# Stacking both directions of a gated linear attention state into one product, and reordering the decays, loads and norms around it

## The chip, the cores and the metric

The kernel runs on one core of a Trainium2 chip. The metric is the device time of one execution in microseconds (us), lower is better. PE is the matrix engine, PEld its weight loads, DVE, ACT and POOL the vector, scalar and general engines, SP the engine whose queue issues most DMAs.

## What is computed

The reference is one step of a two-layer backbone over 2048 latent tokens and 128 context tokens. The part that the change touches is the bidirectional gated linear attention (GLA) of the first layer: four heads, keys of 64, values of 128, a decay per token and key, a state S (64x128) per head and direction. Cut to that part:

```python
def gla_chunked(q, k, v, g, s0):              # one direction
    def step(S, inp):
        qc, kc, vc, gc = inp
        b = jnp.cumsum(gc, axis=2)
        o_inter = jnp.einsum('bhcd,bhde->bhce', qc * jnp.exp(b), S)
        diff = b[:, :, :, None, :] - b[:, :, None, :, :]
        decay = jnp.where(causal, jnp.exp(jnp.where(causal, diff, 0.0)), 0.0)
        att = jnp.einsum('bhid,bhjd,bhijd->bhij', qc, kc, decay)
        o = o_inter + jnp.einsum('bhij,bhje->bhie', att, vc)
        b_last = b[:, :, -1:, :]
        S_new = jnp.exp(b_last)[:, :, 0, :, None] * S + jnp.einsum('bhcd,bhce->bhde', kc * jnp.exp(b_last - b), vc)
        return S_new, o
    ...

o_f, s_f = gla_chunked(q, k, v, gf, s0f)
o_b, s_b = gla_chunked(flip(q), flip(k), flip(v), flip(gb), s0b)
o = rmsnorm(o_f + flip(o_b), gla_onorm)       # per head
y_gla = o * silu(z_gla)
out = concat([y_gla, y_s5]) @ w_out           # then x = x + gate * out, and the next layer's norm
```

## The kernel before

Tokens are cut into 17 tiles of 128: tiles 0 to 15 are latent, tile 16 is the context, which reads no state. The GLA works on tiles as chunks. `run` first does the S5 branch and the input products, then `gla_back` (L913), then `phase4` (L1155), then the second layer.

`gla_back` walks from tile 16 and then from 15 to 1 and computes the backward states. Each step loads keys, decays and values, forms decayed keys (POOL, ACT, DVE), calls `kv_update` (L944) for the key-value product, and adds it to the decayed state (L939, two DVE operations). All 16 backward states stay in SBUF in `self.sb`, 16 KB a partition, in the pool `glac` on the left side, with the first forward state `sf0` (1 KB). A step of `gla_back` is woven with dense products (`zg_pass`, and `glu_pass` with its stores `zg_d` and `ys_d` on POOL's queue).

`kv_update` transposes the decayed keys (L949, two transposes), copies them (L951) and makes four products, one a head, of 64 output columns each (L955). Heads alternate between output partitions 0 to 63 and 64 to 127 by `tile_position=(0, o)`, and two pairs of heads lie one behind the other.

`phase4` runs a loop over the tiles, written by `weave` (L1577): in round i, `gla_chunk(i)` is the main generator, and at each of its nine steps one step is taken of `turn(i-1)` (norm output transposed, L1179, gated, split for the product), `gla_pre(i+1)` (preparation of the next chunk) and `after(i-2)` (output projection by `out_proj`, residual, row norm, `make_h` with eight transposes, L243, and stores). A planner orders the instructions of every engine from this program by a model of their times, so the order on an engine is not the program's; data and buffers are kept consistent by semaphores.

`gla_pre` loads `qk`, `B` (the summed log decays) and `v`, makes the decayed keys `kh`, and with L1035 to L1038 the decayed queries `qh` of both directions, laid out as 64 rows a head and direction. It calls `gla_arg` for levels 0 to 2 and updates the forward state (L1054). `gla_arg` (L987) makes the decay arguments of one level: four POOL operations (L1003 to L1006), an exponential on ACT (L1007) and a DVE product (L1008). The last level is only a product of queries and keys on POOL (L995).

`gla_chunk` (L1057) has eight levels. In a level, four products of 64 rows (L1081) give scores for that distance of tokens, and a copy by mask (L1088) puts them into `att`. The arguments of the level two ahead are issued at each level. Then, per head, come the product with the forward state (L1096), with the backward state (L1097), and with the values (L1098), all into one accumulator; a copy to `gy` (L1100), four squares (L1105), the inverse root on DVE (`rsqrt`, L83: eleven small operations) and the scaling on POOL (L1107). The row norm of `after` has an inverse root of its own (L1195) and scales the row tile on DVE (L1196).

## Time and profile before

| | before |
|---|---|
| median of 3 runs | 2409.3 us (2407.95 to 2409.64) |
| profiled execution, time | 2415.59 us |
| profiled execution, span | 2413.7 us |
| mean granted clock of PE, as a share of full speed | 0.966 |
| PE busy | 2268.3 us, 94% |
| DVE busy | 1659.3 us, 69% |
| ACT busy | 1042.7 us, 43% |
| POOL busy | 867.6 us, 36% |
| DMA | 332.90 MB, mean 138 GB/s |

The span runs from the first to the last instruction. Matmuls are pipelined and their recorded durations overlap, so the cost of a product is read from the start of one instruction to the start of the next. A product of 32-bit floats outside the split form of `mm3` has two records, a transpose has one.

### The profile page before, as it was taken

The numbers are of one execution on the slowest core, as the hardware profiler recorded it, in microseconds if no ns is written. First come the engines' busy times: TensorE is split into PE (matmuls) and PEld (weight loads), VectorE is DVE, ScalarE is ACT, GpSimd is POOL, SyncE is SP. The second block draws the span as 40 slices with busy tenths as digits, with TensorE's granted clock in tenths as the row PEclk, the third lists the DMA queues.
The fourth block names the chain that finished last, engine by engine and source line by source line (L and its number), as shares of the span: only waits on it lengthen the run. The fifth ranks groups of instructions, "written<-read, shape, count | busy, mean of one in ns | idle before, by whom it ended". The sixth has DMA issues, their size and how long they took to land.

```text
span 2413.7 us, 47276 instructions
## 1 busy us (share of the span) xinstructions
PE 2268.3 (94%) x17473; PEld 2108.3 (87%) x17473; DVE 1659.3 (69%) x3916; ACT 1042.7 (43%) x2533; POOL 867.6 (36%) x1348
## 2 busy tenths in 40 slices
PE   7999887888899987999999999999999997999998
PEld 4988787887897876888888999999999997999998
DVE  4997688888866776888887665565344336676765
ACT  3554644343544453455454432233122115565653
POOL 4127165566522227767674021111101102222221
PEclk9999988999999995999999999999999998999999
DMA  9765853343469873333333642245133223222221
GB/s 322 236 210 181 252 162 99 102 132 110 131 212 310 291 232 100 123 119 123 116 115 102 210 120 80 80 138 147 50 93 102 68 69 100 88 89 88 90 69 58
DMA packets 328040, 332.90 MB, mean 138 GB/s; under 512 B 43969, under 2 KB 274977, under 8 KB 327809
## 3 DMA queue, kind: packets, MB, share of 16 engines
q1 hardware_dynamic: 265312, 238.84, 33.1%
q0 software_dynamic: 14384, 48.65, 5.9%
q10 hardware_dynamic: 48112, 42.38, 5.4%
q8 instruction: 138, 2.26, 0.4%
q14 instruction: 94, 0.76, 0.1%
HBM read 223.57 MB, written 106.22 MB: 137 GB/s over the span
## 4 chain that ended last, share of the span: by engine, by line
PE 57%; DVE 8%; issue 4%; DMA 4%; ACT 2%; POOL 2%; SPq 0%; ACTq 0%; POOLq 0%; DVEq 0%
PE psD L100 7%; PE psW L100 7%; PE psW L101 7%; PE psW L102 7%; PE psD L102 7%; PE psD L101 7%; PE psP L1081 3%; PE psW L1510 2%; PE psW L1463 2%; DVE tabs L641 2%; PE psT L1498 2%; PE psP L1098 1%; PE psP L1096 1%; DMA wst<-in_w_in_o_dram 1%; DMA wst<-h_d 1%
## 5 line engine op out<-in xcount | busy, mean ns | idle before, releaser
L100 PE MATMUL psD<-slot,yT 128*128 128x256 f32 x1088 | 318.2, 293 | 1.9 <-ACT yT L1125 1.9
L102 PE MATMUL psD<-slot,yT 128*128 128x256 f32 x1088 | 314.1, 292 | 0.0
L101 PE MATMUL psD<-slot,yT 128*128 128x256 f32 x1088 | 310.7, 286 | 0.0
L101 PE MATMUL psW<-hq,slot 128*128 128x272 f32 x1024 | 293.0, 287 | 0.0
L102 PE MATMUL psW<-hq,slot 128*128 128x272 f32 x1024 | 292.9, 287 | 0.0
L100 PE MATMUL psW<-hq,slot 128*128 128x272 f32 x1024 | 289.1, 287 | 0.0
L100 PE MATMUL psD<-hq,slot 128*128 128x272 f32 x768 | 235.1, 308 | 46.8 <-ACT fo L814 45.8
L101 PE MATMUL psD<-hq,slot 128*128 128x272 f32 x768 | 230.0, 300 | 0.0
L102 PE MATMUL psD<-hq,slot 128*128 128x272 f32 x768 | 229.5, 300 | 0.0
L100 PEld LDWEIGHTS psD<-slot,yT 128*128 128x128 f32 x1088 | 208.1, 191 | 10.0 <-ACT yT L1125 2.0
L102 PEld LDWEIGHTS psD<-slot,yT 128*128 128x128 f32 x1088 | 205.8, 191 | 4.5 <-issue 2.2
L101 PEld LDWEIGHTS psD<-slot,yT 128*128 128x128 f32 x1088 | 208.1, 191 | 1.8
L100 PEld LDWEIGHTS psD<-hq,slot 128*128 128x128 f32 x768 | 151.8, 199 | 55.2 <-ACT fo L814 48.8
L102 PEld LDWEIGHTS psW<-hq,slot 128*128 128x128 f32 x1024 | 193.1, 189 | 0.0
L101 PEld LDWEIGHTS psW<-hq,slot 128*128 128x128 f32 x1024 | 192.5, 188 | 0.0
L100 PEld LDWEIGHTS psW<-hq,slot 128*128 128x128 f32 x1024 | 190.6, 188 | 0.0
L641 DVE SCALAR_TENSOR_TENSOR tabs<-tabs,s5A,tabw 128x16 f32<-128x16 f32 (+2 forms) x384 | 146.8, 447 | 24.9 <-ACT tabw L637 23.5
L101 PEld LDWEIGHTS psD<-hq,slot 128*128 128x128 f32 x768 | 152.1, 198 | 6.4 <-issue 4.7
L102 PEld LDWEIGHTS psD<-hq,slot 128*128 128x128 f32 x768 | 152.1, 198 | 1.0 <-issue 1.0
L1472 DVE CUSTOM_DVE_ANT_0 sc<-psW,amask,sink 128x512 f32<-128x512 f32 (+1 forms) x128 | 93.6, 732 | 84.7 <-PE psT L1498 76.2
L1007 ACT ACTIVATE arg<-arg 128x512 f32<-128x512 f32 x119 | 75.0, 631 | 143.6 <-POOL arg L1006 140.3
L1475 ACT ACTIVATE sc<-sc,nm 128x512 f32<-128x512 f32 (+1 forms) x128 | 90.9, 710 | 87.9 <-DVE nm L1474 74.8
(376 smaller groups left out, 6543.2 us busy)
## 6 DMA issues: line engine op xcount, KB each, us to landing
wst<-h_d SPq DMA_DIRECT2D x96, 272.0 KB
hq<-hl_d SPq DMA_DIRECT2D x40, 544.0 KB
hl_d<-ht POOLq DMA_DIRECT2D x17, 1024.0 KB, 6.7
wada<-in_w_ada_dram SPq DMA_DIRECT2D x32, 512.0 KB
h_d<-hf SPq DMA_DIRECT2D x17, 512.0 KB
x_d<-x ACTq DMA_DIRECT2D x17, 512.0 KB
h_d<-hf ACTq DMA_DIRECT2D x17, 512.0 KB
wst<-h_d SPq DMA_DIRECT2D x34, 256.0 KB
```

Of the source, the lines that this page charges most:

```text
L100: mm(out, lh, rh, start=start, stop=False)
L101: mm(out, lh, rl, start=False, stop=False)
L102: mm(out, ll, rh, start=False, stop=stop)
L641: V.scalar_tensor_tensor(x[:, at(d, m)], x[:, at(d, 0)], turn(0, d, gg), w[:, 1 - j], op0=OP.mult, op1=op)
L1007: nc.scalar.activation(arg, arg, AF.Exp, scale=0.0625)
L1081: nc.tensor.matmul(pv[:, hh, pr, :], ak[o : o + 64, pr, :], aq[o : o + 64, pr, :], start=True, stop=True)
L1096: nc.tensor.matmul(ot, qh[o : o + 64, 0, pr, :], sf[o : o + 64, pr], start=True, stop=False)
L1463: nc.tensor.matmul(out, r32(qs[:, j, h]), kk, start=j == 0, stop=j == 1)
L1472: V.tensor_tensor_reduce(sv, ps, mask, 1.0, sk[:, h : h + 1], op0=OP.add, op1=OP.max, accum_out=m)
L1475: nc.scalar.activation(sv, src, AF.Exp, bias=nm[:, h : h + 1], accum_out=sm[:, h : h + 1])
L1498: nc.tensor.transpose(pt[:, c, :], t[:, 128 * c : 128 * c + 128], self.ident)
L1510: nc.tensor.matmul(po[kv][:, j % 2], r32(VV[:, b, kv]), r32(t[:, x, :, c, :]), start=c + x == 0, stop=c + x == nb)
```

## The change

- The states of both directions lie in one tile: forward at partitions 0 to 63, backward at 64 to 127, four heads side by side. The decayed queries are stacked in the same way, so that a head's product with both states is one product of 128 rows.
- For this `kv_update` puts all four heads at one output position, 0 in `gla_pre` and 64 in `gla_back`. `next_state` multiplies the old state by its decay on POOL and adds the product on DVE.
- `gla_back` keeps two states and stores each to DRAM (`sb_d`) by a DMA on POOL's queue; `state` loads the backward half for the chunk. The pool `glac` is gone.
- `gla_queries` loads queries and decays in the stacked layout with six DMAs a chunk, two chunks ahead.
- `gla_pre` calls `gla_arg` for levels 0 to 3, and `gla_chunk` for the level three ahead; the buffers of levels above 1 are five.
- The head norm (`gla_norm`) is issued in `turn`, in the round after its chunk, and its inverse root has a fifth column for a row tile of `after`, whose scaling (now on ACT), transposes and store are issued there (`rows`). `x1` has three buffers. The sum of squares of a row tile is scaled by 1/8 to share the divisor 128.

```diff
@@ -926,22 +927,32 @@
             nc.gpsimd.tensor_tensor(E, B[:, :, 0:1].to_broadcast([128, 2, 128]), B, op=OP.subtract)
             nc.scalar.activation(E, E, AF.Exp, scale=0.0625)
             nc.vector.tensor_tensor(E, E, k, op=OP.mult)
-            kv = self.kv_update(p, E, v)
+            kv = self.kv_update(p, E, v, 64)
             if i == 16:
...
+                st = p.tile([128, 4, 128], F32, name="bs", tag="bs", bufs=2)
+                nc.sync.dma_start(st[64:128], a["s0"][1])
                 yield
                 continue
-            eb = p.tile([128, 2], F32, name="beb", tag="beb")
-            nc.scalar.activation(eb, B[:, :, 0], AF.Exp, scale=0.0625)
-            for pr in range(2):
-                nc.vector.scalar_tensor_tensor(
-                    self.sb[:, i - 1, pr], self.sb[:, i, pr], eb[:, pr : pr + 1], kv[:, pr], op0=OP.mult, op1=OP.add
-                )
+            eb = p.tile([128, 2, 2], F32, name="beb", tag="beb")
+            for hh in range(2):
+                nc.scalar.activation(eb[64:128, :, hh], B[64 * hh : 64 * hh + 64, :, 0], AF.Exp, scale=0.0625)
+            nst = p.tile([128, 4, 128], F32, name="bs", tag="bs", bufs=2)
+            self.next_state(p, slice(64, 128), nst, st, eb, kv)
+            st = nst
+            nc.gpsimd.dma_start(self.sb_d[i - 1], st[64:128])
             yield
 
-    def kv_update(self, p, kd, v):
+    def next_state(self, p, o, dst, src, eb, kv):
+
+        t = p.tile([128, 4, 128], F32, name="dst", tag="dst", bufs=1)
+        e = eb.rearrange("p a b -> p (a b)")[o].unsqueeze(2).to_broadcast([64, 4, 128])
+        self.nc.gpsimd.tensor_tensor(t[o], src[o], e, op=OP.mult)
+        self.nc.vector.tensor_tensor(dst[o], t[o], kv, op=OP.add)
+
+    def kv_update(self, p, kd, v, o):
 
         nc = self.nc
         pt = self.bank("T", (128, 2, 128))
...
@@ -949,16 +960,11 @@
             nc.tensor.transpose(pt[:, pr, :], kd[:, pr, :], self.ident)
         kt = p.tile([128, 2, 128], F32, name="kt", tag="kt", bufs=2)
         nc.scalar.copy(kt, pt)
-        kv = self.bank("T", (128, 2, 128))
+        kv = self.bank("T", (128, 4, 128))[o : o + 64]
         for h in range(4):
-            pr, o = h // 2, 64 * (h % 2)
+            pr, c = h // 2, 64 * (h % 2)
             nc.tensor.matmul(
-                kv[o : o + 64, pr, :],
-                kt[:, pr, o : o + 64],
-                v[:, h * 128 : h * 128 + 128],
-                start=True,
-                stop=True,
-                tile_position=(0, o),
+                kv[:, h], kt[:, pr, c : c + 64], v[:, h * 128 : h * 128 + 128], start=True, stop=True, tile_position=(0, o)
             )
         return kv
 
...
@@ -980,7 +986,8 @@
         self.ga = {t: Ring(ga, gc) for t in ("qk", "B", "v")}
         self.ga["arg"] = [ga, gb]
         self.gp = self.pool(es, "glap", 2, side="right")
-        self.gs = {}
+        self.ss, self.xrow = self.gp.tile([128, 5], F32, name="oss", tag="oss", bufs=3), None
+        self.gs, self.gq, self.gn = {}, {}, {}
 
     STEPS = (64, 32, 16, 8, 4, 2, 1, 0)
 
...
@@ -995,7 +1002,7 @@
             G.tensor_tensor(st[li], qk[:, 0], qk[:, 1], op=OP.mult)
             return
         nb = 256 // (2 * s)
-        arg = self.ga["arg"][li > 1].tile([128, 2, 256], F32, name="arg", tag="arg", bufs=4 if li > 1 else 2)
+        arg = self.ga["arg"][li > 1].tile([128, 2, 256], F32, name="arg", tag="arg", bufs=5 if li > 1 else 2)
         av = arg.rearrange("p j (b e s) -> p j b e s", e=2, s=s)
         bv = [B[:, d].rearrange("p r (b e s) -> p (r b) e s", e=2, s=s) for d in range(2)]
         rf = bv[0][:, :, 0, s - 1 : s].to_broadcast([128, nb, s])
...
@@ -1019,8 +1026,17 @@
         for j in range(2):
             nc.sync.dma_start(qk[:, j], self.qk_d[256 * j : 256 * j + 256, ts].rearrange("(r p) t -> p r t", p=128))
             nc.sync.dma_start(B[:, j], self.b_d[:, j, :, ts].rearrange("r p t -> p r t"))
+        if i < 16:
+            if i == 0:
+                self.state(0)
+                nc.sync.dma_start(self.sf[0:64], a["s0"][0])
+            st["sf"] = self.sf
         v = st["v"] = self.ga["v"].tile([128, 512], F32, name="v", tag="v", bufs=1)
         nc.sync.dma_start(v, self.v_d[ts, :])
+        if i == 0:
+            self.gla_queries(0)
+        if i < 15:
+            self.gla_queries(i + 1)
         yield
         self.gla_arg(i, 0)
         yield
...
@@ -1030,42 +1046,59 @@
         V.tensor_tensor(kh, kh, qk[:, 1], op=OP.mult)
         yield
         qa = self.ha.tile([128, 2, 2, 272], F32, name="hq", tag="hq").rearrange("p a b c -> p (a b c)")
-        qh, st["att"] = (qa[:, 512 * j : 512 * j + 512].rearrange("p (a b c) -> p a b c", a=2, b=2) for j in range(2))
-        st["qh"] = qh
-        nc.scalar.activation(qh, B, AF.Exp, scale=0.0625)
-        eb = p.tile([128, 2], F32, name="eb", tag="eb")
-        V.tensor_copy(eb, qh[:, 0, :, 127])
-        V.tensor_tensor(qh, qh, qk[:, 0:1].to_broadcast([128, 2, 2, 128]), op=OP.mult)
+        st["att"] = qa[:, 0:512].rearrange("p (a b c) -> p a b c", a=2, b=2)
+        if i < 16:
+
+            qh, qq = self.gq.pop(i)
+            st["qh"] = qh
+            eb = p.tile([128, 2, 2], F32, name="eb", tag="eb")
+            nc.scalar.activation(eb[0:64].rearrange("p a b -> p (a b)"), qh[0:64, :, 127], AF.Exp, scale=0.0625)
+            nc.scalar.activation(qh, qh, AF.Exp, scale=0.0625)
+            V.tensor_tensor(qh, qh, qq, op=OP.mult)
         yield
         self.gla_arg(i, 1)
         yield
         self.gla_arg(i, 2)
         yield
-        sf = st["sf"] = self.sf
+        self.gla_arg(i, 3)
         if i != 15:
-            kv = self.kv_update(p, kh, v)
+            kv = self.kv_update(p, kh, v, 0)
             if i == 16:
...
             else:
-                self.sf = p.tile([128, 2, 128], F32, name="sf", tag="sf", bufs=3)
-                for pr in range(2):
-                    V.scalar_tensor_tensor(self.sf[:, pr], sf[:, pr], eb[:, pr : pr + 1], kv[:, pr], op0=OP.mult, op1=OP.add)
+                self.state(i + 1)
+                self.next_state(p, slice(0, 64), self.sf, st["sf"], eb, kv)
         yield
+
+    def gla_queries(self, i):
+
+        ts = slice(i * 128, (i + 1) * 128)
+        qh, qq = self.gq[i] = [self.gp.tile([128, 4, 128], F32, name=n, tag=n, bufs=3) for n in ("qh", "qq")]
+        for d in range(2):
+            o = slice(64 * d, 64 * d + 64)
+            self.nc.sync.dma_start(qq[o], self.qk_d[0:256, ts].rearrange("(h k) t -> k h t", k=64))
+            for r in range(2):
+                self.nc.sync.dma_start(qh[o, 2 * r : 2 * r + 2], self.b_d[r, d, :, ts].rearrange("(q k) t -> k q t", k=64))
+
+    def state(self, i):
+
+        self.sf = self.gp.tile([128, 4, 128], F32, name="sf", tag="sf", bufs=3)
+        self.nc.sync.dma_start(self.sf[64:128], self.a["s0"][1] if i == 15 else self.sb_d[i])
 
     def gla_chunk(self, i, out):
 
         nc = self.nc
         V, p = nc.vector, self.gp
         st = self.gs[i]
-        v, qh, sf = st["v"], st["qh"], st["sf"]
+        v, qh = st["v"], st.get("qh")
 
         att = st["att"]
         pss = [None, None]
         for li, s in enumerate(self.STEPS):
-            if 2 < li + 2 < 8:
-                self.gla_arg(i, li + 2)
+            if 3 < li + 3 < 8:
+                self.gla_arg(i, li + 3)
             args = st.pop(li)
             if li % 4 < 2:
                 pss[li % 2] = self.pair((2, 2, 2, 128))
...
@@ -1090,24 +1123,32 @@
         po = self.pair((2, 2, 128))
         for h in range(4):
             pr, hh = h // 2, h % 2
-            o = 64 * hh
             ot = po[:, hh, pr]
             if i < 16:
-                nc.tensor.matmul(ot, qh[o : o + 64, 0, pr, :], sf[o : o + 64, pr], start=True, stop=False)
-                nc.tensor.matmul(ot, qh[o : o + 64, 1, pr, :], self.sb[o : o + 64, i, pr], start=False, stop=False)
+                nc.tensor.matmul(ot, qh[:, h], st["sf"][:, h], start=True, stop=False)
             nc.tensor.matmul(ot, att[:, hh, pr], v[:, h * 128 : h * 128 + 128], start=i == 16, stop=True)
         y = p.tile([128, 2, 2, 128], F32, name="gy", tag="gy", bufs=2)
         V.tensor_copy(y.rearrange("p r h v -> p h r v"), po)
-        ss = p.tile([128, 2, 2], F32, name="oss", tag="oss")
+
+        ss, row, self.xrow = self.ss, self.xrow, None
         for h in range(4):
-            pr, hh = h // 2, h % 2
             junk = p.tile([128, 128], BF16, name="oj", tag="oj", bufs=1)
-            nc.scalar.activation(junk, y[:, pr, hh], AF.Square, accum_out=ss[:, pr, hh : hh + 1])
-        rs = self.rsqrt(p, "ors", ss, [128, 2, 2], 128.0)
-        nc.gpsimd.tensor_tensor(y, y, rs.unsqueeze(3).to_broadcast([128, 2, 2, 128]), op=OP.mult)
+            nc.scalar.activation(junk, y[:, h // 2, h % 2], AF.Square, accum_out=ss[:, h : h + 1])
+        self.ss = p.tile([128, 5], F32, name="oss", tag="oss", bufs=3)
+        self.gn[i] = y, ss, row
         out[i] = y.rearrange("p r h v -> p (r h) v")
         del self.gs[i]
         yield
+
+    def gla_norm(self, i):
+
+        p = self.gp
+        y, ss, row = self.gn.pop(i)
+        n = 5 if row else 4
+        rs = self.rsqrt(p, "ors", ss[:, 0:n], [128, n], 128.0)
+        rh = rs[:, 0:4].rearrange("p (r h) -> p r h", r=2).unsqueeze(3).to_broadcast([128, 2, 2, 128])
+        self.nc.gpsimd.tensor_tensor(y, y, rh, op=OP.mult)
+        return row and row + (rs[:, 4:5],)
 
 
     def hq_tile(self, pool=None):
...
@@ -1171,9 +1212,12 @@
             self.split_rows(p, yT, self.ys_d, i)
             zg = p.tile([128, 4, 128], F32, name="zg", tag="zg", bufs=2)
             nc.sync.dma_start(zg, self.zg_d[:, ts].rearrange("(b p) t -> p b t", p=128))
+            row = self.gla_norm(i)
             y = ys.pop(i)
             for _ in range(3):
                 yield
+            rows(row)
+            yield
             pt = self.bank("T", (128, 4, 128))
             for j in range(4):
                 nc.tensor.transpose(pt[:, j, :], y[:, j, :], self.ident)
...
@@ -1183,20 +1227,31 @@
 
         def after(i):
             ts = slice(i * 128, (i + 1) * 128)
-            x = p.tile([128, 1024], F32, name="x1", tag="x1", bufs=2)
+            x = p.tile([128, 1024], F32, name="x1", tag="x1", bufs=3)
             nc.sync.dma_start(x, self.x_src(i))
             if i == 16:
                 gB[0] = self.gate_rows(p, 0, 1)
             yield from self.out_proj(p, yTs.pop(i), ws, gB[0], x)
-            ss = p.tile([128, 1], F32, name="xss", tag="xss", bufs=2)
+            nc.scalar.dma_start(self.x1_d[ts, :], x)
+            if self.xrow:
+                rows(self.xrow)
+
             junk = p.tile([128, 1024], BF16, name="sqj", tag="ot", bufs=2)
-            nc.scalar.activation(junk, x, AF.Square, accum_out=ss)
-            nc.scalar.dma_start(self.x1_d[ts, :], x)
-            rs = self.rsqrt(p, "rs1", ss, [128, 1], 1024.0)
-            V.tensor_scalar(x, x, rs, None, op0=OP.mult)
+            nc.scalar.activation(junk, x, AF.Square, scale=float(np.sqrt(0.125)), accum_out=self.ss[:, 4:5])
+            self.xrow = (i, x)
+            if i == 16:
+                rows(self.xrow)
+            yield
+
+        def rows(row):
+
+            if not row:
+                return
+            i, x, *rs = row
+            rs = rs[0] if rs else self.rsqrt(p, "ors", self.ss[:, 4:5], [128, 1], 128.0)
+            self.tc.keep_in_program_order(nc.scalar.activation(x, x, AF.Copy, scale=rs))
             h, _ = self.make_h(1, 1 if i == 16 else 0, x, two)
-            nc.scalar.dma_start(self.h1_d[:, :, ts], h)
-            yield
+            nc.scalar.dma_start(self.h1_d[:, :, i * 128 : (i + 1) * 128], h)
 
         slot = prefetch()
         self.weave(NTILE, lambda i: self.gla_chunk(i, ys), turn, after, lambda i: self.gla_pre(i + 1) if i < 16 else iter(()))
...
@@ -1617,11 +1672,6 @@
                     for _ in dense:
                         pass
                 eR = es.enter_context(ExitStack())
-                c = self.pool(eR, "glac", 1, side="left")
-                self.sb = c.tile([128, 16, 2, 128], F32, name="sb")
-                self.sf = c.tile([128, 2, 128], F32, name="sf0")
-                self.nc.sync.dma_start(self.sb[:, 15], a["s0"][1])
-                self.nc.sync.dma_start(self.sf, a["s0"][0])
                 with ExitStack() as e1:
                     zg = self.col_slots(ring, a["w_in_e"], 1056, 512)
                     dense = self.zg_pass(hq, zg)
```

## Rows read from the trace of the kernel before

**Rows 1.** The page: busy us, share of the span, instructions

```profile
PE 2268.3 (94%) x17473; PEld 2108.3 (87%) x17473; DVE 1659.3 (69%) x3916; ACT 1042.7 (43%) x2533; POOL 867.6 (36%) x1348
```

**Rows 2.** Busy by stretch: from:to, length, engines (count), granted clock, DMA share, GB/s

```profile
720.00:822.00 102.00, 101.72 (x783) 82.32 (x782) 68.32 (x147) 49.61 (x122) 25.57 (x44) 1.00 0.93 300
896.65:957.12 60.47, 39.76 (x217) 31.59 (x215) 41.19 (x77) 24.22 (x50) 43.76 (x83) 0.59 0.38 115
984.77:1301.43 316.66, 315.82 (x2607) 275.04 (x2608) 271.73 (x640) 162.07 (x402) 220.32 (x402) 1.00 0.38 120
```

**Rows 3.** Waits from 1000 to 1300: us in total, times, longest

```profile
ACT arg L1007 <- POOL arg L1006: 101.6, 67, 2.6
POOL arg L1003 <- PE psP L1081: 71.5, 19, 6.2
...
PE psP L1076 <- DVE hq L1088: 0.5, 1, 0.5
```

**Rows 4.** Chain of waits from 1150 to 1180: shares by line

```profile
by line: PE psD L100 16.9%; PE psP L1081 15.8%; PE psD L102 15.2%; PE psD L101 14.1%; PE psP L1096 11.1%; PE psP L1098 9.8%; PE psP L1097 6.0%; PE psT L955 3.9%; PE psT L243 3.4%; PE psT L1179 2.0%; PE psT L949 1.2%; PE psP L1076 1.1%
```

**Rows 5.** DVE in order of time, L1100: start, us, instruction

```profile
984.77 0.69 DVE L1100 COPY gy<-psP 128x512 f32<-128x512 f32 x1 [0.73 <-PE psP L1098]
...
1301.43 0.69 DVE L1100 COPY gy<-psP 128x512 f32<-128x512 f32 x1
```

**Rows 6.** PE in order of time: output products of one head

```profile
1055.52 0.48 PE L1096 MATMUL psP<-sf,hq 64*128 64x128 f32 x2
1055.85 0.38 PE L1097 MATMUL psP<-sb,hq 64*128 64x128 f32 x2
1056.16 0.49 PE L1098 MATMUL psP<-v,hq 128*128 128x128 f32 x2
1056.58 0.48 PE L1096 MATMUL psP<-sf,hq 64*128 64x128 f32 x2
```

**Rows 7.** PE in order of time: output products of the context tile

```profile
1321.41 1.05 PE L1098 MATMUL psP<-v,hq 128*128 128x128 f32 x8
1322.21 0.37 PE L102 MATMUL psD<-slot,yT 128*128 128x256 f32 x1
```

**Rows 8.** Chain of waits, pieces in order of time: start, us, what

```profile
1159.16 1.09 PE psP L1081 x16
...
1173.64 0.59 PE psT L955 x8
```

**Rows 9.** By line and shape, 1000 to 1300: count, busy us, mean ns, idle before

```profile
L1196 DVE TENSOR_SCALAR x<-x,rsy 128x1024 f32<-128x1024 f32 x12 | 10.9, 912 | 0.0
L92 DVE SCALAR_TENSOR_TENSOR rst<-rsy 128x1 f32<-128x1 f32 x36 | 8.1, 224 | 0.4
L1193 ACT ACTIVATE sqj<-x 128x1024 bf16<-128x1024 f32 x12 | 12.7, 1057 | 31.1 <-DVE x L1151 31.1
L1107 POOL TENSOR_TENSOR gy<-gy,rsy 128x512 f32<-128x512 f32 x12 | 14.4, 1198 | 11.4 <-DVE rsy L94 11.4
```

**Rows 10.** POOL in order of time, and POOL's busy time on `arg` by stretch

```profile
1048.54 0.90 POOL L1003 TENSOR_TENSOR arg<-B 128x128 f32<-128x128 f32 x1
1049.40 0.40 POOL L1004 TENSOR_TENSOR arg<-B 128x128 f32<-128x128 f32 x1
...
984.77:1301.43 316.66, 187.38 (x364) 1.00 0.38 120
```

**Rows 11.** DMA queues, 900 to 1330: packets, MB, share of 16 engines

```profile
q1 hardware_dynamic: 43781, 33.19, 25.8%
```

**Rows 12.** The loop's start: PE, POOL, SP in order of time; a wait of SP

```profile
902.41 2.08 PE L1081 MATMUL psP<-arg 64*128 64x128 f32 x16 [5.47 <-DVE tzs L887]
907.53 0.61 POOL L1028 TENSOR_TENSOR kh<-B 128x256 f32<-128x256 f32 x1 [4.05 <-ACT slot L219]
908.75 0.47 SPq L1021 DMA_DIRECT2D B<-b_d  x1
SPq L1119 <- DMA ys_d<-gzs: 5.0, 1, 5.0
```

15 lines of the change are left out of this document (8 added, 7 removed).

## The prediction

> **What bounds the kernel now.** I read the page's busy line first: TensorE 94% of the span [rows 1]. That is an average, so the next view is the busy time by stretch around the code that changes [rows 2]. Three stretches matter. From 720 to 822 us (the backward pass `gla_back`, woven with dense products) PE is busy 101.7 of 102.0 us. From 984.8 to 1301.4 (the loop of `phase4` in steady state) it is busy 315.8 of 316.7, and the granted clock is 1.00. Between them, from 896.7 to 957.1, it is busy only 39.8 of 60.5 with a mean granted clock of 0.59: the loop's start. The waits of the steady stretch [rows 3] say that POOL and ACT wait a lot (ACT for POOL 101.6 us, POOL for PE 71.5 us), but the longest wait of PE itself is 0.5 us. The chain of one tile [rows 4] consists of PE lines alone. So in the loop one tile costs its PE instructions and nothing else. Its length: the copy `gy` starts at 984.77 and, 13 tiles later, at 1301.43 [rows 5], so (1301.43 - 984.77)/13 = 24.36 us a tile. Whatever takes PE time out of a tile comes off the total; an earlier issue of something for which PE doesn't wait is worth nothing there.
>
> **Output products, the gain.** Per head, before, L1096 and L1097 (64 rows each, forward and backward state) and L1098 (128 rows) follow one another. The same head's start recurs from 1055.52 to 1056.58 [rows 6]: 1.06 us, of which L1096 0.33, L1097 0.31, L1098 0.42. Four heads: 4.24 us. After, a head has two products of 128 rows. The context tile shows that shape already: four L1098 back to back from 1321.41 to 1322.21 [rows 7], 0.80, or 0.20 each. Eight of them are 1.60; I add 0.10 for the change to the 64-row products of L1081 that follow (L1098 costs 0.42 before a 64-row product, 0.32 less 0.10 otherwise): 1.70. Gain 4.24 - 1.70 = 2.54 us in each of 16 latent tiles, **-40.6 us**. The stacked operand needs queries and states of both directions at partitions 0 to 63 and 64 to 127, which the new loads provide; no PE work is added for that.
>
> **State update, the price.** `kv_update` has four products of 64 output columns. Before, heads alternate between column positions 0 and 64, and L955 is on the chain with 0.59 us for the four [rows 8]. After, all four have one position. The trace doesn't show four products in one narrow position, so I bound it. From below: four at 0.20 [rows 7] plus 0.10 for the change of shape = 0.90, +0.31. From above: four at the 0.32 of consecutive products in one row half [rows 6] plus 0.10 = 1.38, +0.79. Less than nothing is excluded, since the same four products and the same transposes remain and only their overlap goes. Nearest row: eight L1081 (16 records, two a product) over two row halves take 1.09 [rows 8], so the four that share a half take 1.09 one after another; with 0.10 that is 1.19, +0.60. I take this value, since there too narrow products follow one another in one part of the array. There are 16 calls in the loop (tile 15 has none) and 16 in the backward pass, which is PE-bound too [rows 2]: 32 x 0.60 = **+19.2 us** (9.9 to 25.3).
>
> The Trainium skill (TensorE: Matmul & The Clock Gate, Part 3) says that small products run side by side when they lie in distinct column groups. That speaks against this edit; by it 0.59 would at most double, an estimate of +0.59 a call and +19 in all. The trace shows only the alternating form.
>
> **Vector work, covered.** DVE loses the row tile's own inverse root (eleven operations on one column, 0.22 for the first of a round [rows 9], some 2.1 us), the scaling L1196 (0.91), the copy of `eb`, and trades two state updates for one add of the same size: from 20.9 us a tile (271.7/13 [rows 2]) to about 17.8. ACT gains the scaling (1.06, as a pass over as many elements, L1193 [rows 9]) and a second small exponential: 12.5 to about 13.8. POOL gains the state's product (64x512, priced as the 128x512 of L1107, 1.20 [rows 9]): 16.9 to 18.1. The new tile is 24.36 - 2.54 + 0.60 = 22.4 us of PE, so all three stay below it, POOL nearest with 81%. Cost 0 while that holds. In `gla_back` the same POOL product and a store on POOL's queue wait for DVE's add, and behind them stand the `zg_d` and `ys_d` stores that free buffers of the dense products; POOL is busy 25.6 of 102 us there [rows 2]. I take 0, up to +4.
>
> **Moved steps.** The head norm goes to the next chunk: eleven DVE operations and POOL's multiply of `y`, which now stands between that chunk's POOL operations and must precede its four transposes on PE, with three steps of slack. The row norm goes about two chunks on, with an ACT pass, eight transposes, eight ACT copies and the `h1_d` store on ACT's queue; a third `x1` buffer holds the longer life. None of it was waited for by PE [rows 3], so 0 in the loop. At its end the rows of the last tiles come later, beside the next phase's products: 0, up to +3. SP gets seven more loads a tile, queued among `qk`, `B`, `v`; the transfers add 640 KB a tile to a queue that takes 25.8% of the DMA engines here [rows 11]; 0. New short waits of PE, since its slack against POOL shrinks by 3 us a tile: +1, up to +8. Decays three levels ahead: 0 in the loop, something at the start.
>
> **The start.** At 902.41 PE runs two levels of chunk 0 [rows 12]; POOL's next operation, `kh`, starts only at 907.53 after 4.05 us idle, while SP's next load waits 5.0 us for the last `ys_d` store: I read this as a buffer of the pass before that still occupies the space. From there POOL works without a break and PE lives on what it delivers. After, 17 KB of states leave the left side and the loop's pools grow by some 19 KB on the right, at the end that holds queries, states and norms. So `kh` and the decays from level 2 on should no longer overlap that buffer, and four decay levels of chunk 0, not two, can be ready at 902: two levels at about 2.2 us (four POOL operations of 0.51, 187.4/364 [rows 10], with ACT and DVE behind them), `kh`, and part of the 5 us gap, about -8. If everything of chunk 0 is early, 5 + 5 x 2.2 + 2 = -18; if the first states and queries, 13 loads on SP, are late by what they need to issue (13 x 0.47 [rows 12]), +6. I take **-8**.
>
> **Sum.** -40.6 + 19.2 - 8 + 1 = -28.4 us. The profiled execution took 2415.6 us (span 2413.7), 6 above the median of the runs, and would become 2387.2; the median 2409.3 becomes **2381**. With kv at its low end and the best start 2409.3 - 40.6 + 9.9 - 18 = 2361; with kv dear (+25.3), the start unchanged and 4 for waits, 2398.
>
> **Rivals.**
> - *The feed falls behind.* With 22.4 us of PE a tile, POOL (81%), its arguments through ACT and DVE arrive late at some levels: ACT waits for POOL 67 times already. 1.0 us a tile takes back 16: with half the gain at the start, -40.6 + 19.2 + 16 - 4 = -9.4, 2400. Against it: the buffers go from four to five and the lead from two to three levels.
> - *The loop doesn't shorten*, since another chain holds a tile at 24.4: then the backward pass's +9.6 and the start's -8 remain, 2411. Against it: the chain of a tile shows no other engine [rows 4].
> - *POOL becomes the bound (slower).* Its decay operations L1003 to L1006 take 0.40 at one time and 0.90 at another, when DVE works beside them [rows 10]; the mean is 0.51 of POOL's time each, 28 a tile, 14.4 us. The rest of its tile is 16.9 - 14.4 + the new 1.2 = 3.7. Slower than before needs a tile of 24.4 + 0.6 (the backward pass must be paid as well) = 25.0, so (25.0 - 3.7)/28 = 0.76 us each; with all at 0.85 a tile is 27.5, 16 x 3.1 = +50 and +9.6 - 8 beside it: 2461. For it: a shorter tile packs DVE and POOL closer. Against it: DVE loses 3 us a tile.
>
> The Trainium skill (SBUF — State Buffer, section "SBUF: two separate sides") states such a lock between POOL and DVE operations with two SBUF inputs. The two durations agree with that.
> - *A still better start with cheap state updates*: below 2360.
>
> **How the numbers follow.** Forecast 0.70, better than that 0.05, feed behind 0.12, no shorter loop 0.07, POOL bound 0.06. A measurement of this kernel can tell about 0.2% (5 us) from no change. Faster by more: 0.70 + 0.05 + 0.10 of the feed case = 0.85; within: 0.02 + 0.07 = 0.09; slower: 0.06. The range takes in the forecast's ends and the feed case: 2360 to 2402.
>
> **What would show it.** Right: `gy` copies about 22.4 us apart; eight products of 128 rows in about 1.7 us; L955 at about 1.2 us; PE waits in the loop under 1 us a tile; the backward pass about 10 us longer; the first `gy` copy earlier than 937.5 relative to the pass before. Wrong: a tile above 23.5 with PE waiting for DVE or POOL; 64-column products that cost no more than 0.59 or more than 1.4; PE at half clock far beyond the 50 us of before.

## The result and the profile after

The changed kernel takes 2427.1 us (2422.8 to 2429.6) against 2408.7 us (2408.0 to 2409.6) of the kernel before, run beside it: a ratio of 1.0075, 95% interval 1.0057 to 1.0092. It is slower by 0.75%, where 2381 was forecast.

The page after, span and busy time, beside [rows 1]:

```profile
span 2421.0 us, 47146 instructions
...
PE 2245.2 (93%) x17345; PEld 2100.5 (87%) x17345; DVE 1650.8 (68%) x3697; ACT 1060.8 (44%) x2580; POOL 891.1 (37%) x1393
```

PE is still busiest, at 93%. As before, the stages say more. Columns are the stretch, its length, busy time and records of PE, PEld, DVE, ACT and POOL, granted clock, DMA share, GB/s. The first two rows answer [rows 2] (pass of the backward states; start of the loop), the third is the loop, the stretch of [rows 3].

```profile
core 0: us, PE busy (x) PEld busy (x) DVE busy (x) ACT busy (x) POOL busy (x), PEclk, DMA share, GB/s
720.00:822.00 102.00, 94.64 (x671) 79.41 (x670) 60.70 (x107) 45.85 (x113) 43.01 (x66) 0.98 0.90 294
913.50:947.10 33.60, 16.40 (x100) 13.78 (x99) 25.64 (x42) 12.25 (x26) 20.53 (x38) 0.62 0.54 162
1000.00:1300.00 300.00, 285.08 (x2424) 256.64 (x2425) 245.56 (x454) 164.18 (x399) 212.09 (x403) 0.99 0.47 139
```

In the pass PE is busy 94.6 of 102.0 us, where it was 101.7; in the loop 285.1 of 300. In both PE now waits for something. Waits of the loop, 1000 to 1300 us (engine, line, what was waited for: us in total, times, longest), against [rows 3], where the longest wait of PE was 0.5:

```profile
PE psP L1114 <- DVE rst L92: 5.3, 3, 2.4
PE psP L1114 <- DVE rsy L94: 3.2, 4, 1.7
PE psP L1114 <- DVE hq L1121: 2.2, 3, 1.0
...
ACT eb L1055 <- DMA qh<-b_d: 21.7, 10, 3.1
...
ACT qh L1056 <- DMA qh<-b_d: 4.3, 7, 1.3
...
DVE rsv L89 <- ACT oj L1136: 16.7, 8, 3.2
```

PE waits up to 2.4 us, for DVE, and never for POOL. Two rows are new: ACT stands 26.0 us at the exponent of the query decays (L1055, L1056) until their loads land, and DVE 16.7 us at the first operation of an inverse root until ACT's squares (L1136) are there. The third and the sixteenth `gy` copy, the pair of [rows 5], after:

```profile
992.51 0.69 DVE L1131 COPY gy<-psP 128x512 f32<-128x512 f32 x1 [0.18 <-PE psP L1129]
...
1301.94 0.68 DVE L1131 COPY gy<-psP 128x512 f32<-128x512 f32 x1
```

(1301.94 - 992.51)/13 = 23.80 us a tile, against 24.36 before and 22.4 forecast. PE is busy 95.0% of it, 22.6 us, near the 22.4 forecast, and 1.2 us a tile are waits.

The next table cuts each profiled execution at five marks into four stages: the end of the S5 products (L738 in the kernel before, L739 after), the last GLU product, the first and last `gy` copy, the last product of the next phase's query, key and value pass. All times are us, good to about 0.3; "tile" is worked out as above. The second row is the change; the others belong to the experiments.

| kernel | pass | start | loop | end | sum | tile | ratio to before (95%) |
|---|---|---|---|---|---|---|---|
| before | 193.0 | 41.1 | 385.0 | 280.8 | 899.9 | 24.36 | 1 |
| after | 211.6 | 33.6 | 376.8 | 290.5 | 912.5 | 23.80 | 1.0075 (1.0057 to 1.0092) |
| e1_row | 212.1 | 33.6 | 375.9 | 280.7 | 902.3 | 23.88 | 1.0034 (1.0021 to 1.0047) |
| e2_actq | 212.1 | 36.4 | 391.9 | 290.7 | 931.1 | 24.40 | 1.0145 (1.0130 to 1.0160) |
| e3_pad | 204.0 | 35.8 | 377.7 | 291.2 | 908.7 | 23.55 | 1.0058 (1.0041 to 1.0075) |
| e4_back | 201.9 | 30.0 | 377.1 | 288.8 | 897.8 | 23.94 | 0.9998 (0.9988 to 1.0008) |
| g1_pin | 212.9 | 33.4 | 360.7 | 290.1 | 897.1 | 22.76 | 0.9996 (0.9986 to 1.0005) |
| g2_noload | 212.4 | 36.8 | 357.6 | 289.0 | 895.8 | 23.08 | 0.9995 (0.9983 to 1.0007) |
| g3_norm | 214.9 | 33.6 | 376.8 | 280.5 | 905.8 | 23.95 | 1.0022 (1.0012 to 1.0032) |
| f3_both | 198.4 | 30.0 | 376.5 | 280.2 | 885.1 | 23.98 | 0.9952 (0.9936 to 0.9967) |
| h1_pinboth | 198.1 | 29.8 | 367.9 | 280.2 | 876.0 | 23.52 | 0.9912 (0.9891 to 0.9934) |
| h2_pad | 190.9 | 31.5 | 376.8 | 280.6 | 879.8 | 23.31 | 0.9913 (0.9896 to 0.9930) |
| h3_dveback | 205.8 | 32.1 | 368.5 | 289.9 | 896.3 | 23.47 | 1.0003 (0.9990 to 1.0015) |
| h4_fwd | 189.8 | 37.1 | 379.4 | 280.1 | 886.4 | 23.80 | 0.9953 (0.9935 to 0.9971) |
| j1_hybrid | 198.2 | 29.8 | 361.3 | 283.5 | 872.8 | 22.69 | 0.9888 (0.9868 to 0.9908) |
| j2_hybfwd | 198.6 | 33.0 | 362.6 | 283.5 | 877.7 | 23.15 | 0.9896 (0.9875 to 0.9917) |
| j3_hybpad | 192.9 | 30.5 | 373.4 | 282.1 | 878.9 | 22.63 | 0.9900 (0.9879 to 0.9921) |
| j4_hybdve | 204.8 | 31.4 | 362.4 | 280.4 | 879.0 | 23.05 | 0.9918 (0.9904 to 0.9933) |

The two profiled executions differ by 7.3 us, less than the medians (18.5), since that of before lay 6 above its median and that of after 4 below. In the four stages the change costs 12.6 us: pass +18.6, start -7.5, loop -8.2, end +9.7. The rest of the span, code that no kernel here changes, took 1513.8 before, 1508.5 after and 1507 to 1517 in the others, so differences of a few us in it mean nothing. Single runs far above all others (9816 us once for j1_hybrid, 4272 and 2494 for the kernel before) are left out.

### The profile page after: what moved, and what is told of

The parts are those of the page before. It is cut to its first block, busy times and chain, and to the rows that moved or that the text cites. A ratio compares the mean times of both kernels' runs of the same rounds, so it can differ in the third digit from the quotient of the medians.

```text
span 2421.0 us, 47146 instructions
## 1 busy us (share of the span) xinstructions
PE 2245.2 (93%) x17345; PEld 2100.5 (87%) x17345; DVE 1650.8 (68%) x3697; ACT 1060.8 (44%) x2580; POOL 891.1 (37%) x1393
## 4 chain that ended last, share of the span: by engine, by line
PE 51%; DVE 7%; DMA 5%; issue 4%; ACT 3%; POOL 2%; SPq 2%; ACTq 0%; POOLq 0%; DVEq 0%
PE psW L100 7%; PE psW L102 7%; PE psW L101 7%; PE psD L100 6%; PE psD L101 6%; PE psD L102 5%; PE psW L1565 2%; PE psW L1518 2%; PE psT L1553 2%; DMA qh<-b_d 1%; PE psP L1114 1%; DVE tabs L642 1%; SPq L1083 1%; DMA zr<-z_d 1%; DVE hq L1121 1%
## 5 line engine op out<-in xcount | busy, mean ns | idle before, releaser
L100 PE MATMUL psD<-slot,yT 128*128 128x256 f32 x1088 | 317.3, 293 | 2.4 <-ACT yT L1166 2.4
L100 PE MATMUL psW<-hq,slot 128*128 128x272 f32 x1024 | 289.1, 287 | 0.0
L100 PE MATMUL psD<-hq,slot 128*128 128x272 f32 x768 | 234.5, 307 | 50.8 <-ACT fo L815 43.7
L100 PEld LDWEIGHTS psD<-slot,yT 128*128 128x128 f32 x1088 | 209.1, 192 | 9.7 <-ACT yT L1166 2.4
L100 PEld LDWEIGHTS psD<-hq,slot 128*128 128x128 f32 x768 | 150.5, 197 | 64.3 <-ACT fo L815 46.1
L100 PEld LDWEIGHTS psW<-hq,slot 128*128 128x128 f32 x1024 | 190.5, 188 | 0.0
L248 ACT ACTIVATE hf<-psT,msh,msc 128x128 f32<-128x128 f32 x272 | 101.0, 464 | 44.5 <-PE psT L244 44.5
```

Source lines behind the costliest of these rows:

```text
L100: mm(out, lh, rh, start=start, stop=False)
L248: nc.scalar.activation(f[:, k, :], pt[:, j, :], AF.Identity, bias=sh, scale=sc)
```

## The experiments

Three stages went wrong, so there are three questions: what takes the loop's gain, what lengthens the pass, what lengthens the end. The kernels are cut from the changed one, one part at a time, and later combined.

**The row norm put back (e1_row).** Scaling and inverse root stand again at the end of `after`, on DVE, with two `x1` buffers.

```diff
-            rows(row)                                  # in turn, three steps on
...
+            rs = self.rsqrt(p, "rs1", ss, [128, 1], 1024.0)   # in after
+            V.tensor_scalar(x, x, rs, None, op0=OP.mult)
```

> The changed kernel with one part undone: the row norm of `after` is again issued at the end of `after`, with an inverse root of its own and the scaling on DVE, and `x1` has two buffers. Queue theory: in the loop the load of `x` on SP's queue waits 98 us in 300 for a buffer that the later row norm holds, the loads of `qh` stand behind it, ACT waits 26 us for them, and DVE and PE behind ACT. Then the 16 tiles from the first to the last `gy` copy fall from 377 to about 360 us, the gap from the last `gy` copy to the end of the qkv products falls from 291 to 281, and the median from 2427 to about 2400 (2392 to 2408). Slack theory (POOL and DVE can't feed a tile of 22 us in time, whatever the queues): the loop stays at 372 to 380, only the end gains, median 2415 to 2420.

The time was 2418.9. SP's wait at the `x` load fell from 98 us to 30 in 1000 to 1300, ACT still stood 25.5 us at the exponents, and the loop stayed (375.9 for 376.8): that load, standing ahead of the query loads, is not what the loop waits for. The whole gain lies in the end, 280.7 for 290.5. ACT after, behind the last chunk, with SP's next weight loads:

```profile
1332.49 1.15 ACT L1252 ACTIVATE x<-x,rsy 128x1024 f32<-128x1024 f32 x1 [2.21 <-DVE rsy L94]
...
1335.59 2.90 ACT L248 ACTIVATE hf<-psT,msh,msc 128x128 f32<-128x128 f32 x8 [1.95 <-PE psT L244]
1338.35 1.18 ACT L1252 ACTIVATE x<-x,rsy 128x1024 f32<-128x1024 f32 x1
...
1340.93 2.94 ACT L248 ACTIVATE hf<-psT,msh,msc 128x128 f32<-128x128 f32 x8
...
1348.68 1.14 ACT L220 CAST slot<-wst 128x512 fp32r<-128x512 f32 x2 [4.81 <-PE psD L102]
1350.05 13.20 SPq L219 DMA_DIRECT2D wst<-in_w_in_o_dram  x8
```

The last row tiles' scalings (L1252) and the copies of their transposes (L248) stand on ACT from 1332 to 1344; the next weight casts (L220) come at 1348.7, after 4.81 us more in which ACT waits for a product of the output projection, and the weights behind them load from 1350. The first product of the next phase (first and last start in us), after:

```profile
L100 PE MATMUL psW<-slot,zh x408: 280/283/581, 1358.6 to 1614.4; 128*128 128x256 f32 x136
```

and with the row norm put back:

```profile
L100 PE MATMUL psW<-slot,zh x408: 278/283/388, 1341.8 to 1607.7; 128*128 128x256 f32 x136
```

It starts 16.8 us earlier. So the end's 10 us are the moved row norm; which of the waits on ACT passes them on was not taken apart.

**Query loads on ACT's queue (e2_actq).** All six are issued by `nc.scalar` in place of `nc.sync`.

```diff
-            self.nc.sync.dma_start(qq[o], ...
+            self.nc.scalar.dma_start(qq[o], ...       # the same for qh
```

> The changed kernel with the six loads of decayed queries issued from ACT's queue, so that they stand behind no load of `x`. Queue theory: the loop falls from 377 to about 362 us although the row norm is where the change put it, the end stays as it is, median about 2412 (2406 to 2420). Slack theory: loop 372 to 382, and ACT's queue work makes it no better, median 2425 to 2432.

2444.9, the loop 391.9. ACT's wait at the exponents halved (13.9 us of 300) and others came: PE stood 10.5 us at the output projection (L100) for ACT's cast of `yT`, and the first tile took 27.1 us for 19.6. The issues themselves now stand in ACT's stream, each at its buffer. It doesn't separate the theories of the loop; it shows that ACT's stream is the wrong place for the loads.

**Less room for early work (e3_pad).** 13 KB a partition stand unused on the left side during the pass, so that fewer of the loop's buffers exist there.

```diff
                 with ExitStack() as e1:
+                    self.pool(e1, "pad", 1, side="left").tile([128, 3328], F32, name="pad")
```

> The changed kernel with 13 KB a partition left unused below the pools of the pass before the loop, about where the states stood, so that the space of chunk 0's decays and keys is again taken until that pass ends. Early-work theory (loads and POOL operations of chunk 0 that now start during the pass delay that pass): the last product of the pass ends at about 905 instead of 913.6, and the first `gy` copy comes 36 to 40 us after it instead of 33.5; median 2420 to 2427. Price theory (the pass is longer by its own products, states and stores alone): the pass still ends at 912 to 915 and the start gets longer, median 2430 to 2437.

2422.4. The pass fell by 7.6 us, so the loop's early loads and decays do cost the pass. But the first tile of the loop took 29.7 us for 19.6, and of the 7.6 us 3.8 are left in the sum of the stages, and the time shows no more than that (2422.4 for 2427.1, with ratios whose intervals overlap).

**The backward update as before (e4_back).** Products in alternating column positions, two DVE operations, states stored in two halves.

```diff
-            kv = self.kv_update(p, E, v, 64)
+            kv = self.kv_pair(p, E, v)                 # tile_position=(0, o), o = 64 * (h % 2)
-            self.next_state(p, slice(64, 128), nst, st, eb, kv)
+            for pr in range(2):
+                nc.vector.scalar_tensor_tensor(nst[:, pr], st[:, pr], eb[:, pr : pr + 1], kv[:, pr], ...)
```

> The changed kernel with the backward pass as before: products at alternating columns, state update by two DVE operations, no POOL product; each state is still stored to DRAM by POOL's queue, in two halves. Price theory: four products fall from 1.02 to 0.59 us, 16 x 0.43 = 7 us, and with the POOL products gone the pass ends 8 to 16 us earlier (898 to 905), median 2411 to 2419. Early-work theory: only the 7 us of products come back, of which the transfers hide a part, the pass ends at 907 to 911, median 2420 to 2425.

2409.5. The pass fell by 9.7 us, within the 8 to 16 of the price theory, and the start by 3.6, which it hadn't foreseen; the time is 1.5 below its range.

Neither e1_row nor e2_actq had named what the loop waits for, so two theories stood next. *Load theory*: the planner places the exponent of the query decays on ACT right behind their loads; the loads come later than it thinks, and ACT, in order, holds back everything behind. *Vector theory*: the head norm's inverse root, now between the next chunk's decays, holds DVE.

**Loads taken away (g2_noload).** One chunk's queries and decays are loaded and used for all; the loads of the other 15 are left out.

```diff
+        if i == 0: (the six loads, into qs and qq)
-            nc.scalar.activation(qh, qh, AF.Exp, scale=0.0625)
+            nc.scalar.activation(qh, self.q0[0], AF.Exp, scale=0.0625)
```

> The changed kernel with the query and decay loads of one chunk only, used for all 16 latent chunks: six loads on SP's queue a tile are gone (so the output products take wrong queries from the second chunk on; all instructions of the engines remain). Load theory: in the loop ACT stands 26 us of 300 at the exponent of freshly loaded decays, the squares behind it are late, DVE stands behind the squares and PE behind DVE (14.9 us of 300 idle); with no load to wait for, the loop from the first to the last gy copy falls from 376.8 to 358 to 364 us and the time from 2427 to 2409 to 2415. Vector theory: PE's waits name the inverse root of the head norm, which stands between the next chunk's decays on DVE whatever the loads do; the loop stays at 372 or more, the time at 2422 or more.

2410.7, the loop 357.6, as the load theory said (358 to 364). The vector theory falls: every DVE operation is still there. ACT isn't free of waiting at the exponent, though: it stands there 15.5 us of 300 until the output products that read the same buffer are done, and DVE still waits 18.3 us for the squares. So the length of these two waits is not the price by itself.

**Head norm put back too (g3_norm).** e1_row with `gla_norm`'s inverse root and product back at the chunk's end.

> The changed kernel with the head norm back at the end of its own chunk (its own inverse root, scaling on POOL right behind) and the row norm back at the end of the row tile, as in the kernel before; stacked products, loads and three levels of lead stay. Its neighbour is the run with the row norm alone put back (2418.9, loop 375.9). Vector theory: the loop falls from 375.9 to 358 to 364, the time to 2401 to 2407. Load theory: ACT still stands at the exponents, the loop stays within 3 us of 375.9, the time within 4 of 2418.9.

2418.3, the loop 376.8; ACT still stands 26.1 us at the exponents. Within the bounds of the load theory, and the place of the head norm is worth nothing here.

**The exponents held (g1_pin).** The same work and the same loads; the two exponents stay at their written place.

```diff
-            nc.scalar.activation(qh, qh, AF.Exp, scale=0.0625)
+            self.tc.keep_in_program_order(nc.scalar.activation(qh, qh, AF.Exp, scale=0.0625))   # and eb
```

> The changed kernel with the two exponents of the queries (eb, qh) held at their written place on ACT, two steps behind the chunk's first decays, instead of where the planner puts them, which is right behind the loads. Load theory: the loads have landed by then, ACT's wait of 26 us of 300 falls below 8, the loop from 376.8 to 360 to 368, the time to 2411 to 2419. Vector theory: ACT's wait goes, the loop stays at 372 or more.

2410.9, the loop 360.7, a tile 22.76. In its waits from 1000 to 1300 the rows of the query decays are gone from ACT:

```profile
PE psP L1114 <- DVE rsy L90: 1.2, 2, 0.9
PE psP L1129 <- DVE hq L1121: 1.1, 2, 0.9
...
ACT arg L1014 <- POOL arg L1013: 77.0, 54, 3.7
ACT x L1252 <- DVE rsy L94: 21.7, 12, 3.1
```

and PE is busy 293.2 of 300 (columns as in the windows above):

```profile
1000.00:1300.00 300.00, 293.17 (x2526) 263.20 (x2525) 256.90 (x478) 170.20 (x415) 220.04 (x405) 1.00 0.48 143
```

The exponent of chunk 10, 66 us ahead of the chunk's `gy` copy in the changed kernel, is 25 us ahead of it here. One place in one queue was worth 16 us.

**Two prices undone at once (f3_both).** e1_row and e4_back in one kernel.

> The changed kernel with two parts undone at once: the backward state update as in the kernel before, and the row norm at the end of its own row tile. If the two prices are independent places (the pass of the backward states, and the weight casts behind the loop), the gains add: 2427.1 - 17.7 - 8.2 = 2401 (2398 to 2405), faster than the kernel before by 0.3%. If the row norm at the loop's end and the state update lean on the same thing (the room that the loop's pools leave), less than half of the smaller gain is added: 2406 or more.

2401.8, as the sum said (2401): pass and end are separate places.

**All three mended (h1_pinboth).** f3_both with the exponents held.

> Three parts mended at once: the backward state update as in the kernel before, the row norm at the end of its own row tile, and the queries' exponents held at their written place. Loop (360.7 with the exponents held), weight casts behind it (-10) and the pass before it are three places, so the gains should add: 2401.8 - 16 = 2386 (2382 to 2390). If the row norm's scaling and inverse root on DVE (90% busy in the loop with them, 82 to 86% without) take the place of the loads as the loop's second limit, the loop stays at 368 or more and the time at 2392 or more.

2390.8, between the two cases, with the loop at 367.9, 7 above g1_pin. DVE is what differs, third of the busy times:

```profile
1000.00:1300.00 300.00, 281.21 (x2478) 256.63 (x2477) 277.99 (x612) 154.59 (x401) 215.33 (x382) 0.99 0.48 144
```

278.0 of 300 us busy, for 256.9 in g1_pin, which leaves the row norm to ACT.

**The same with less early room (h2_pad).**

> The last kernel with 13 KB a partition held unused on the left side during the pass of the backward states, so that fewer buffers of the coming loop exist there. If early loads and decays of the coming loop cost the pass time beside the state update (pass 201.9 with the old update, 193.0 before), the pass falls by 5 to 8 us, and the time to 2379 (2376 to 2383). If the 7.6 us that the same room saved with the new update were that update's own contention, the pass stays within 2 us and the time within 3 of the run without it.

The pass fell by 7.2 us, to 190.9, below that of before; the time stayed (2389.9) where 2379 was expected. The first two tiles of the loop took 54.6 us for 42.7. So what the early decays cost in the pass is paid later where they are forbidden, in nearly the same amount.

**The update of the pass on DVE, columns as changed (h3_dveback).**

```diff
-            self.next_state(p, slice(64, 128), nst, st, eb, kv)
+            for h in range(4):
+                nc.vector.scalar_tensor_tensor(nst[64:128, h], st[64:128, h], eb[64:128, ...], kv[:, h], ...)
```

> The changed kernel with one edit: in the pass of the backward states the update is four operations on DVE with the decay as a scalar, not a product on POOL and a sum on DVE; products in one column position, states stacked, loads and norms as changed. POOL theory: the product on POOL's in-order queue holds back stores of the dense products, the pass falls from 211.6 by 4 us or more, the time to 2423 or below. Column theory: what the old update gained (9.7 us) is mostly 16 x 0.43 us of the four products themselves, the pass stays within 3 of 211.6, the time at 2424 to 2429.

2411.2, as the POOL theory said, but by more than it asked for. The pass fell by 5.8 us, PE in it from 94.6 to 99.3 busy of 102:

```profile
720.00:822.00 102.00, 99.27 (x728) 84.59 (x727) 72.83 (x154) 50.44 (x123) 31.78 (x59) 0.98 0.94 309
```

So the update with POOL's product costs the pass 5.8 us more than the same update on DVE. That it is the stores held behind the product was not shown: POOL's wait for the new state at the `sb_d` store grew, from 4.9 to 9.8 us. The loop fell by 8.3 too, in code that this edit doesn't touch; its planner's order differs, ACT stands 21.6 us of 300 at the exponents for 26.0, and why it is better was not separated. So an order alone can move the loop by 8 us.

**Forward products in alternating columns (h4_fwd).** h2_pad with `kv_pair` in the loop, its sum in two halves on DVE.

```diff
-        self.nc.vector.tensor_tensor(dst[o], t[o], kv, op=OP.add)
+        for hh in range(2):
+            w = [z[o].rearrange("p (r q) v -> p r q v", q=2)[:, :, hh] for z in (dst, t)]
+            self.nc.vector.tensor_tensor(w[0], w[1], kv[64 * hh : 64 * hh + 64], op=OP.add)
```

> The kernel with all parts mended and the room held, with the forward update's four products in alternating column positions too, their sum as two operations on DVE of half the size. Price theory: four products cost 1.02 us in one position and 0.59 in two, so 16 x 0.43 = 7 us go while PE bounds the loop: 6 to 8 below the run without it, 2372. If DVE or POOL bounds the loop by now, it stays within 2 us of that run.

2399.4, 9.5 above h2_pad, beyond both cases. In the stages 2.6 us of it lie in the loop, where DVE is busy 279 of 300 us and the sum takes it twice 0.41 us for 0.67; that fits DVE as the bound, 16 x 0.15 = 2.4. The start has 5.6 more, and why was not separated.

**Row norm moved, but not for the last tiles (j1_hybrid).** h1_pinboth with the row norm on ACT as in the change for tiles 0 to 12, and at its own end for 13 to 16.

> The exponents held at their written place, the backward update as in the kernel before, and the row norm moved as in the changed kernel, but for row tiles 13 to 16, which are scaled on DVE at their own end. DVE theory: the row norm on DVE bounds the loop of the run with all three mended (367.9); moved, the loop is at 358 to 363, the weight casts start as early as with the norm put back (end 280 to 283), the time is 2390.8 - 7 = 2383 (2379 to 2386). If PE's own feed through POOL and ACT bounds it, the loop stays at 366 or more and the time at 2388 or more.

2384.5, the loop 361.3, the end 283.5, as the DVE theory said but for 0.5 us of the end. From 1000 to 1300 us:

```profile
1000.00:1300.00 300.00, 294.54 (x2539) 265.82 (x2538) 255.04 (x487) 175.63 (x435) 206.89 (x379) 1.00 0.50 150
```

PE 294.5, DVE 255.0. It is the fastest kernel here, 1.1% below the kernel before.

**Forward columns once DVE has room (j2_hybfwd).**

> The last kernel with the forward update's four products in alternating column positions and their sum as two operations of half the size on DVE. Price theory: DVE has room now, so 16 x 0.43 = 7 us less of PE show: 4 to 8 below the last kernel, 2377. If DVE or the feed still bounds the loop, no gain: 0 to 8 above it.

2386.9: no gain. The four products do take 0.59 us again, for 1.02, and PE's busy time fell from 294.5/300 of 22.69 = 22.28 us a tile to 284.0/300 of 23.15 = 21.91; PE now waits for the cast of `yT` on ACT:

```profile
1000.00:1300.00 300.00, 283.99 (x2491) 256.62 (x2492) 252.14 (x480) 175.23 (x423) 204.03 (x383) 0.99 0.48 146
...
PE psD L100 <- ACT yT L1192: 10.1, 10, 1.1
```

That this wait took the gain is likely, not shown: j4_hybdve below has it too (11.3 us), and as little busy time of PE (284.3 of 300, 21.85 a tile), with four products of 1.02.

**Less early room with PE as the bound (j3_hybpad).**

> The hybrid kernel with 13 KB a partition held unused on the left in the pass of the backward states. There the pass fell by 7 us and the loop took 9 more, as if the feed counted from the end of the pass. With DVE less full: if PE bounds the loop, the pass's 7 us are kept and the time is 2376 (2373 to 2379); if the feed (decays through POOL, ACT, DVE) bounds it, they are given back and the time is within 3 us of the hybrid kernel.

2388.6, 4.1 above the hybrid kernel, in runs that spread over 10 us: given back again. The pass fell by 5.3 us and the first tile took 31.5 us for 20.6.

**Stacked states kept, three small mends (j4_hybdve).**

> The changed kernel with three small mends that keep its stacked states and its single column position: exponents held at their written place, row tiles 13 to 16 normed at their own end, and the backward update as four operations on DVE. Pass 205.8 as in the run with that update alone, start 32, loop 361, end 281, the rest 806, 703 ahead of the pass: 2390 (2386 to 2394); 6 us above the hybrid kernel, since the backward pass still pays 16 x 0.43. If the update on POOL was what hid in the loop's gain of that run (368.5), the loop falls below 358 and the time below 2386.

2392.8, as forecast (2390; pass 204.8, loop 362.4, end 280.4).

## Why the prediction was wrong

Terms of the sum, in the stages of the table:

| term | forecast | measured |
|---|---|---|
| output products | -40.6 | -37.6 |
| four products in one column position, 32 times | +19.2 | +13.8 |
| start | -8 | -7.5 |
| waits in the loop (measured: what is left) | +1 (up to +8) | +22.5 |
| the rest of the pass (measured: what is left) | 0 (up to +4) | +11.7 |
| end | 0 (up to +3) | +9.7 |
| sum | -28.4 | +12.6 |

The two marked terms are not read from rows: they are what the loop and the pass changed by, less the products. In the loop, the 1.2 us a tile in which PE stands make 19 of the 22.5. The prediction's own sign of being wrong, "a tile above 23.5 with PE waiting for DVE or POOL", is what came: 23.80, with PE waiting for DVE.

**Output products: right.** The first two and the last of seven products of one tile after, back to back (start, length), beside [rows 6]:

```profile
1035.49 0.38 PE L1129 MATMUL psP<-v,hq 128*128 128x128 f32 x2
1035.71 0.39 PE L1128 MATMUL psP<-sf,qh 128*128 128x128 f32 x2
...
1036.83 0.39 PE L1129 MATMUL psP<-v,hq 128*128 128x128 f32 x2
```

From 1035.49 to 1036.83 they follow each other at 0.223 us. Eight and the change of shape are 1.89, for 1.70 forecast from [rows 7]: 16 x (4.24 - 1.89) = 37.6.

**State update: right in kind, priced 5.4 us too high.** On the chain after (start, time on the chain):

```profile
1159.80 1.02 PE psT L966 x8
```

1.02 for the four products, where they took 0.59 in alternating positions [rows 8]: +0.43 a call, inside the bounds of 0.31 to 0.79, and 32 x 0.43 = 13.8. The calls of the pass take the same times (medians). The nearest row (L1081) gave 0.60 and was too dear a guide. The Trainium skill (TensorE: Matmul & The Clock Gate, Part 3) says that small products in distinct column groups run side by side; the trace agrees, with a factor of 1.73 where the prediction's estimate from it was at most two.

**The start: right in size.** 33.6 for 41.1. What wasn't seen is that the early work isn't free: e3_pad, h2_pad and j3_hybpad each take 5 to 8 us out of the pass by forbidding some of it, and the loop's first tiles give half of it back in the first and all of it in the other two.

**The loop: the step "Moved steps".** It said that SP's loads and the moved operations cost nothing, "None of it was waited for by PE", and listed what PE waits for. It didn't ask what stands behind each new wait on its own engine. The new loads of the decayed queries are waited for by ACT. One such place after, in order of time (start, length, engine, and in brackets the idle time before it and what ended it):

```profile
1113.84 2.53 SPq L1083 DMA_DIRECT2D qh<-b_d  x3
...
1116.10 0.62 ACT L1014 ACTIVATE arg<-arg 128x512 f32<-128x512 f32 x1
...
1118.93 0.21 ACT L1055 ACTIVATE eb<-qh 64x4 f32<-64x4 f32 x1 [2.21 <-DMA qh<-b_d]
1120.42 0.63 ACT L1056 ACTIVATE qh<-qh 128x512 f32<-128x512 f32 x1 [1.28 <-DMA qh<-b_d]
1120.95 1.65 ACT L1014 ACTIVATE arg<-arg 128x512 f32<-128x512 f32 x3
1121.08 0.90 DVE L1057 TENSOR_TENSOR qh<-qh,qq 128x512 f32<-128x512 f32 x1 [2.09 <-ACT qh L1056]
1121.90 0.72 DVE L1121 COPY_PREDICATED hq<-mk,psP 128x512 f32<-128x512 uint8 x1
...
1122.76 1.23 PE L1114 MATMUL psP<-arg 64*128 64x128 f32 x8 [2.45 <-DVE rst L92]
```

SP issues the last three loads of `qh` from 1113.84 to 1116.37. ACT has finished a level's exponents at 1116.72 and then stands 2.21 and 1.28 us at the exponents of `qh`, with three decay levels behind them; they run only from 1120.95. DVE idles 2.09 us, its mask copy of the level comes at 1121.90, and PE, which needs the buffer that this copy frees (the row names the operation just behind it, which ends last before PE starts), idles 2.45. The exponent that holds ACT belongs to a chunk whose output products come three tiles later (three buffers of `qh`, and the load follows the chunk that frees one); nothing on PE was in need of it. g2_noload takes the loads away and g1_pin only moves the exponent; they return the loop to 358 and 361, so the early exponent, held by its loads, is shown as the cause, for 16 to 19 of the 22.5 us. As the planner orders each kernel anew, and an order alone moved the loop by 8 us in h3_dveback, one run would be thin; but the four kernels with the exponents held, the row norm on ACT for all or most tiles and no room forbidden (g1_pin, j1_hybrid, j2_hybfwd, j4_hybdve) lie at 360.7 to 362.6, and all with the exponents where the planner sets them and their loads kept at 368.5 or above. The lead in the code is real, but the planner spends it: it loads as soon as a `qh` buffer falls free and sets the exponent right behind the load.

The rival "the feed falls behind" had the size, 1.0 us a tile (measured 1.2), and the wrong place: it spoke of POOL's arguments, and POOL's product of the decays was ready; PE has no wait for POOL in the loop. The rival "POOL becomes the bound" did not come: POOL is busy 212 of 300 us, 71%. DVE, estimated at 17.8 us a tile, is busy 245.6/300 x 23.80 = 19.5. Once ACT no longer stands, the row norm on DVE is the next bound (h1_pinboth, 367.9, against j1_hybrid, 361.3), so that move of the change is worth 7 us in the loop.

**The pass: the step "In gla_back ... I take 0, up to +4".** It was costed at nothing with stores on POOL's queue as its only risk. h3_dveback, which takes the product off POOL, returns 5.8 us. The longest rows of POOL's waits and PE's longest, 705 to 900 us after:

```profile
PE psD L100 <- DVE fo L835: 6.2, 3, 3.9
...
POOL zg_d L836 <- DVE fo L835: 43.0, 18, 5.5
POOL ys_d L890 <- DVE gzs L889: 32.4, 14, 8.9
...
POOL sb_d L945 <- DVE bs L953: 4.9, 4, 1.9
```

POOL doesn't wait for the new sum long (4.9 us at the `sb_d` store), so the store that waits for DVE isn't the main price; PE waits 6.2 us for `fo`, which DVE makes (2.5 in h3_dveback). The granted clock isn't it: from 705 to 895 us it is 0.99 in both kernels. With the old update and the early work held back, the pass is at 190.9 and 192.9, as before (193.0), although the states are still stored to DRAM there: those stores have no price of their own. So products, POOL and early work explain all of its +18.6; how the 11.7 divide between the last two isn't exact, since e3_pad's 7.6 and h3_dveback's 5.8 make 13.4.

**The end: the step "At its end the rows of the last tiles come later ... 0, up to +3".** It named the place and took PE's view of it. The scalings went to ACT, and ACT is the engine that casts the next phase's weights; e1_row and f3_both, which put the row norm back, return 10 us.

With these places mended and the backward update as before, the hybrid kernel is at 0.9888 of the kernel before, 27 us, about the gain that was forecast for the change as a whole (28.4). That the two agree is partly chance, as this kernel doesn't pay for the one column position in the pass, which the forecast had at 9.6; j4_hybdve, which does, is at 0.9918, 20 us.
